# A third weight chunk by seven products, its turns shared with the down-projection, in a float32 decoder layer on one core

## The chip, the cores and the metric

One Trainium2 chip, one of its cores. The metric is the device time of one execution in microseconds (us); lower is better. A core has TensorE (PE, matrix products into PSUM banks), VectorE (DVE), ScalarE (ACT), GpSimd (POOL) and SyncE (SP, which here only starts transfers). They run their own instruction streams, each in its own order, and meet through semaphores.

## The reference

A decoder layer for 256 tokens of width 1024, all in float32:

```python
h = rms_norm(x, norm1_g[l])
proj = h @ w_in[l]                       # attention q, k, v and the convolution's input
...
x = x + jnp.concatenate([attn, conv], axis=-1) @ w_out[l]
h = rms_norm(x, norm2_g[l])
x = x + (jax.nn.silu(h @ w_gate[l]) * (h @ w_up[l])) @ w_down[l]
```

`w_gate` and `w_up` are 1024 x 2816, `w_down` is 2816 x 1024. The change lies in the last line.

## The kernel before

**Products.** Each float32 operand is held as a high part (`h`, the rounded value) and a low part (`l`, the rest). `product` makes three matmuls of 128 x 128 by 128 x 512: high by high, high by low, low by high. Weights come from memory as blocks of 128 x 2048 float32 (`raw`, 1 MB, four buffers) and are split in pieces of 1024 columns: ScalarE writes the high half (`wh`, L256), VectorE the low half (`wl`, L265), into seven pairs of buffers. `feed(at + LEAD)` keeps the split some four pieces ahead of the products. When a block's second piece is split, `load_next` starts the next load on SP's queue.

**Chunks.** The 2816 columns of gate and up are cut in six chunks: five of 512 and chunk 3 of 256. A plain chunk of 512 takes 8 units of 4 products (two token halves, two halves of the contraction, gate and up): 32 products. A unit uses one piece, and all of a chunk's gate or up goes to two banks (`fg`). A *shared* chunk sees tokens by contraction halves (A11 to A22) and weights (b11, b21 of gate, b12, b22 of up) as 2 x 2 matrices and multiplies them with seven block products in place of eight: 7 units of 4 products, into the banks U, V and W. For that, sums of the tokens' blocks (`xs`) are formed once, and sums of weight blocks on the way: VectorE adds b12 and then b22 to b11 (`raw<-raw,raw`, L255, four instructions a chunk), and POOL's queue adds b22 to b12 and b21 to b11 by accumulating transfers (L268). So a shared chunk has 14 pieces. Its b11, b12 and b22 have homes of their own (`big_h`, `big_l`, `side`), b21 a `raw` buffer.

**Order.** `STAGES = ((0,), (1, 2), (3,), (4, 5))`: chunk 0 plain; chunk 1 shared, its units in turns with plain chunk 2; chunk 3; chunk 4 shared, in turns with plain chunk 5. Then come the 22 row tiles of the down-projection, four products a row with one piece, into the four banks pd00 to pd11; the last four rows (`LAST`) are done bank by bank. TensorE's order is that of the code; a task list (`spawn`, `step`, one step each two products) puts the work on finished banks in between: `gate2_task` and `up2_task` for plain chunks (silu on ScalarE, then `ac`, the product with it, on VectorE at L796), and `turned` (four transposes `aT` on TensorE at L787, the high part on ScalarE at L790, the low part `lo` on VectorE at L792).

**Banks.** There are eight: four under `mm`, two under `s`, two under `t`, each dealt out in turn. Before, `fg` and W come from `mm`, U and V from `s`, transposes from `t`; of the pd banks two come from `s` and two from `mm`.

Of the kernel before, what the change touches and what calls it, by code (L numbers as in the profile page):

```python
# [16 lines left out]
P = 128  # L17
# [47 lines left out]
STAGES = ((0,), (1, 2), (3,), (4, 5))  # L65


def _halves(c):

    if c:  # L70
        return [(z, kh, half) for z in range(2) for kh in range(2) for half in range(2)]
    return [(z, kh, half) for kh in range(2) for z in range(2) for half in range(2)]


def _plan():

    base = 14
    block = {}
    for c, width in enumerate(WIDTHS):
        for z in range(2 if width == W else 1):  # L80
            for kh in range(2):
                block[c, z, kh] = base
                base += 1
    loads = [(i, "raw") for i in range(2, 14)]
    plain = lambda i: [(i, a, None, "load") for a in range(2)]
    sources = [p for i in range(14) for p in plain(i)]
    for stage in STAGES:
        second = [(block[stage[-1], z, kh], half) for z, kh, half in _halves(stage[-1])
                  if (stage[-1], z, kh) in block]
        second_pieces = [(i, half, None, "load")  # L90
                         for j, (i, half) in enumerate(second)]
        second_loads = [(i, "raw") for i, half in second if half == 0]
        if len(stage) == 1:
            loads += second_loads
            sources += second_pieces
            continue
        b11, b21, b12, b22 = (block[stage[0], z, kh] for z in range(2) for kh in range(2))
        loads += [(b11, "big_h"), (b12, "big_l"), second_loads[0], second_loads[1], (b22, "side"),
                  (b21, "raw")] + second_loads[2:]
        both = [(0, 1) for _ in range(7)]  # L100
        todo = [(b11, None, None), (b11, b12, (b12, b22)), (b11, b22, (b11, b21)), (b21, None, "load"),
                (b12, None, None), (b22, None, None), (b11, None, None)]
        for j in range(8):
            if j < 7:
                i, add, then = todo[j]
                sources += [(i, a, add, then) for a in range(2)]
            sources.append(second_pieces[j])
    for i in range(base, NB):
        loads.append((i, "raw"))
        sources += plain(i)  # L110
    return loads, sources
# [66 lines left out]
def _build(nc, tc, t, ctx):  # L178
# [18 lines left out]
    def load(pl, name, shape, eng=nc.sync, **kw):  # L197
        tl = pl.tile(shape, F32, name="c_" + name, **kw)
        eng.dma_start(tl, t[name])
        return tl  # L200
# [21 lines left out]
    loads, sources = _plan()  # L222

    def load_next():
        while loads:
            i, home = loads.pop(0)
            if home == "raw":
                r = raw.tile([P, BW], F32, name=f"raw{i}", tag="raw")
            else:
                r = (late_pool[0] if home == "side" else keep).tile([P, BW], F32, name=f"raw{i}", tag=home)  # L230
            nc.sync.dma_start(r, t["w"][i - 2])
            blocks[i] = r
            if home == "raw":
                return
# [14 lines left out]
    def feed(upto):  # L249
# [8 lines left out]
        while waiting and waiting[0][2] <= upto:  # L258
            dst, src, j = waiting.pop(0)
            i, a, add, then = sources[j]  # L260
            if then == "low":
                nc.scalar.activation(dst[1], dst[0].bitcast(F32), AF.Copy, scale=-1.0)
                nc.gpsimd.dma_start(dst[1].bitcast(F32), src, accum_op=ALU.add)
            else:
                nc.vector.tensor_tensor(dst[1], src, dst[0].bitcast(F32), op=ALU.subtract)  # L265
            if type(then) is tuple:
                to, more = then
                nc.gpsimd.dma_start(blocks[to][:, cut(a)], t["w"][more - 2][:, cut(a)], accum_op=ALU.add)  # L268
            if then in ("load", "low") and a:
                load_next()  # L270
# [42 lines left out]
    g1 = load(const, "g1", [P, KT], nc.scalar)  # L313
# [36 lines left out]
    for kt in range(KT):  # L350
# [9 lines left out]
        if kt == 1:  # L360
            load_next()
            rope = load(early, "rope", [P, NT, 2 * HD])
            gqk = load(early, "gqk", [P, 2, 2 * HD])
# [6 lines left out]
    ident = load(const, "ident", [P, P])  # L370
    load_next()
    taps = load(early, "taps", [96, 324], tag="Y", bufs=3)
    dwr = early.tile([96, W], F32, name="dwr", tag="Y", bufs=3)
    nc.sync.dma_start(dwr, t["dw_w"])
    mask = load(early, "mask", [P, 3 * P])
# [18 lines left out]
    def tables_task():  # L394
# [12 lines left out]
        G["glub"] = load(early, "glub", [P, 2, W])  # L407
        G["cols"] = load(const, "cols", [P, 16])
# [307 lines left out]
    def residual_task(i, n):  # L716
        cols = slice(n * W, n * W + W)
        nc.vector.tensor_tensor(x2[:, i, cols], po[i, n], x2[:, i, cols], op=ALU.add)
        sq = ffn["late"].tile([P, W], F32, name=f"sq{i}{n}", tag="sum", bufs=5)
# [50 lines left out]
    acts = late.tile([P, 2, NF, T], F32R, name="act")  # L770

# [32 lines left out]
    def up2_task(c, banks, width):  # L804
        ups = []
        for i in range(NT):
            ups.append(times(c, i, banks[i][:, W - width:] if width < W else banks[i], ffn["s", c][i], width))
            yield 1
        for i in range(NT):
            yield from turned(c, i, ups[i], width // P)  # L810

    def part(name):
        return late.tile([P, W], F32, name=name, tag="sum", bufs=5)

    xs = [acts[:, z, NF - 8:, :].rearrange("p f (b q) -> p (f b) q", b=2).rearrange("p (s k) q -> p s k q", s=4)
          for z in range(2)]

    def xsums_task():
# [3 lines left out]
        for j, (p, q, op) in enumerate(((A21, A22, ALU.subtract), (s[0], A11, ALU.subtract),  # L822
                                        (A11, A21, ALU.subtract), (A12, s[1], ALU.add))):
            nc.vector.tensor_tensor(s[j], p, q, op=op)
        yield 1
        for j in range(4):
            nc.scalar.activation(xs[0][:, j], s[j], AF.Copy)
        yield 2
        for j in range(4):
            nc.vector.tensor_tensor(xs[1][:, j], s[j], xs[0][:, j].bitcast(F32), op=ALU.subtract)  # L830
# [36 lines left out]
    xsum = lambda j: [[z[:, j, k, :] for z in xs] for k in range(4)]  # L867

    def plain_units(c):

        banks = {}

        def unit(z, kh, half):
            if kh == half == 0:
                banks[z] = [mm_bank(f"fg{c}{z}{i}") for i in range(NT)]
            for k in (2 * half, 2 * half + 1):
                if k % 2 == 0:
                    feed(at[0] + LEAD)
                for i in range(NT):
                    product(banks[z][i], [a[:, 4 * kh + k, tok(i)] for a in g], wpart(at[0], k % 2),  # L880
                            kh == k == 0, kh == 1 and k == 3)
            at[0] += 1
            if kh == half == 1:
                spawn((gate2_task, up2_task)[z](c, banks[z], W), EVICT)

        return [lambda z=z, kh=kh, half=half: unit(z, kh, half) for z, kh, half in _halves(c)]

    def shared_units(c):

        U, V = (t_bank(f"{n}{c}", "s") for n in "UV")  # L890
        banks = {"U": U, "V": V}

        def unit(lhs, name, start, stop, after):
            if name == "W":
                banks["W"] = mm_bank(f"W{c}")
            for k in range(4):
                if k % 2 == 0:
                    feed(at[0] + LEAD)
                product(banks[name], lhs[k], wpart(at[0], k % 2), start and k == 0, stop and k == 3, not start)
                at[0] += k % 2  # L900
            if after:
                spawn(after(), EVICT)

        todo = ((block(0, 0), "U", True, True, lambda: copied("s1", U)),
                (xsum(0), "V", True, True, lambda: copied("s5", V)),
                (xsum(1), "U", False, True, lambda: copied("s2", U)),
                (block(1, 0), "W", True, True, lambda: gate_first(c, banks["W"])),
                (xsum(2), "U", False, True, lambda: up_second(c, U)),
                (xsum(3), "V", False, True, lambda: up_first(c, V)),
                (block(1, 1), "U", False, True, lambda: gate_second(c, U)))  # L910
        return [lambda u=u: unit(*u) for u in todo]
# [3 lines left out]
    at = [at]  # L915
    for stage in STAGES:
        if len(stage) == 2:
            first, second = shared_units(stage[0]), plain_units(stage[1])
            for j in range(8):
                if j < 7:  # L920
                    first[j]()
                second[j]()
        elif WIDTHS[stage[0]] == W:
            for u in plain_units(stage[0]):
                u()
        else:
            c = stage[0]
            banks = [mm_bank(f"fg{c}{i}") for i in range(NT)]
            for k in range(KT):
                if k % 2 == 0:  # L930
                    feed(at[0] + k // 2 + LEAD)
                for i in range(NT):
                    product(banks[i], [a[:, k, tok(i)] for a in g], wpart(at[0] + k // 2, k % 2), k == 0, k == KT - 1)
# [75 lines left out]
```

## Time and profile before

| | |
|---|---|
| median of 3 runs | 294.79 us (294.23 to 295.06) |
| profiled execution | 294.38 us, span 292.4 us |
| TensorE | 285.6 us busy, 1333 matmuls |
| VectorE | 213.1 us busy, 326 instructions |
| ScalarE | 174.1 us busy, 262 instructions |
| transfers | 60.73 MB, 208 GB/s over the span |

Times in the profile are us from the span's start. A duration of a matmul contains part of its neighbour's, since TensorE overlaps them; the chain of waits lists each stretch of work on the path to the end once, with its time. `aT<-c_ident,ac` reads: written `aT`, from `c_ident` and `ac`. `[0.87 <-DVE ac L796]` is idle time of the engine just before, and what ended it.

### The profile page before, as it was taken

What the parts mean: (1) busy time and instruction counts of PE and PEld (TensorE: products, weight loads), DVE (VectorE), ACT (ScalarE), POOL (GpSimd) and SP (SyncE); (2) the same over time, 40 slices, a digit from 0 to 9 for tenths busy, and PEclk for the clock granted to TensorE, in tenths of its full rate; (3) what the DMA queues carried; (4) which work ended last, traced back from release to release, by engine and by line L of the source; (5) the groups of instructions that cost most, each with busy time, mean ns of one, the idle gap of its engine ahead of it and who ended that gap; (6) DMA issues with size and microseconds to landing.
All of it is one profiled execution on the core that took longest, in us unless ns stands there. A gap on an engine that the chain in (4) does not pass through costs nothing.

```text
span 292.4 us, 3667 instructions
## 1 busy us (share of the span) xinstructions
PE 285.6 (98%) x1333; PEld 231.6 (79%) x1333; DVE 213.1 (73%) x326; ACT 174.1 (60%) x262; POOL 21.4 (7%) x42
## 2 busy tenths in 40 slices
PE   8999999999999999997999999999999999999994
PEld 6888877778688888885888888888888888888883
DVE  3899995999972957999987758997787574544111
ACT  5776768989825778655967454597856263343000
POOL 0005372000000000021100001120000000000000
PEclk9999999999999999999999999999999999999999
DMA  7999868533703439299961993899335368400012
GB/s 250 416 411 364 337 250 308 210 143 146 288 0 143 146 108 429 84 388 240 213 266 45 427 422 119 143 244 320 132 133 189 133 226 323 164 2 0 0 48 96
DMA packets 11475, 60.73 MB, mean 208 GB/s; under 512 B 1537, under 2 KB 2145, under 8 KB 5698
## 3 DMA queue, kind: packets, MB, share of 16 engines
q1 hardware_dynamic: 9874, 54.86, 49.1%
q0 software_dynamic: 1440, 5.64, 9.5%
q8 instruction: 10, 0.16, 0.2%
q14 instruction: 7, 0.06, 0.1%
q10 hardware_dynamic: 144, 0.00, 0.0%
HBM read 59.46 MB, written 1.05 MB: 207 GB/s over the span
## 4 chain that ended last, share of the span: by engine, by line
PE 84%; DVE 10%; ACT 2%; issue 2%; DVEq 0%; ACTq 0%
PE pd L708 21%; PE p L669 18%; PE fg L708 18%; PE po L708 7%; PE U L708 7%; PE V L708 3%; DVE wl L265 3%; PE W L708 2%; DVE raw L255 2%; PE aT L787 2%; PE warm L326 1%; PE S L512 1%; PE pT L542 1%; ACT wh L256 1%; DVE g L735 1%
## 5 line engine op out<-in xcount | busy, mean ns | idle before, releaser
L265 DVE TENSOR_TENSOR wl<-raw,wh 128x1024 fp32r<-128x1024 f32 x102 | 122.7, 1221 | 24.4 <-ACT wh L256 24.0
L256 ACT ACTIVATE wh<-raw 128x1024 fp32r<-128x1024 f32 x102 | 105.9, 1056 | 46.3 <-PE pd L708 19.9
L708 PE MATMUL fg<-wh,g 128*128 128x512 f32 x224 | 72.8, 392 | 0.0
L708 PE MATMUL pd<-wh,act 128*128 128x512 f32 x176 | 55.2, 391 | 0.0
L708 PEld LDWEIGHTS fg<-wh,g 128*128 128x128 f32 x224 | 42.0, 188 | 8.6
L708 PE MATMUL fg<-wl,g 128*128 128x512 f32 x112 | 43.6, 389 | 0.0
L708 PEld LDWEIGHTS pd<-wh,act 128*128 128x128 f32 x176 | 33.0, 188 | 6.9
L708 PE MATMUL pd<-wl,act 128*128 128x512 f32 x88 | 34.2, 389 | 0.0
L669 PE MATMUL p<-wh,xh 128*128 128x512 f32 x80 | 32.9, 412 | 0.0
L669 PE MATMUL p<-wh,xl 128*128 128x512 f32 x80 | 31.3, 392 | 0.0
L669 PE MATMUL p<-wl,xh 128*128 128x512 f32 x80 | 26.5, 392 | 0.0
L708 PEld LDWEIGHTS fg<-wl,g 128*128 128x128 f32 x112 | 21.1, 188 | 4.2
L708 PEld LDWEIGHTS pd<-wl,act 128*128 128x128 f32 x88 | 16.5, 188 | 3.3
L669 PEld LDWEIGHTS p<-wh,xh 128*128 128x128 f32 x80 | 15.1, 189 | 3.7 <-issue 0.7
L669 PEld LDWEIGHTS p<-wl,xh 128*128 128x128 f32 x80 | 15.1, 189 | 3.1 <-DVE wl L265 0.2
L669 PEld LDWEIGHTS p<-wh,xl 128*128 128x128 f32 x80 | 15.1, 188 | 3.1
L790 ACT ACTIVATE act<-aT 128x512 fp32r<-128x512 f32 (+1 forms) x12 | 6.7, 561 | 17.9 <-PE aT L787 17.9
L268 POOL DMA_DIRECT2D raw<-w x8 | 7.0, 879 | 141.4 <-DVE raw L255 86.4
L792 DVE TENSOR_TENSOR act<-aT,act 128x512 fp32r<-128x512 f32 (+1 forms) x12 | 7.7, 644 | 11.4 <-ACT act L790 11.4
L948 DVE TENSOR_TENSOR o<-pd,x 128x512 f32<-128x512 f32 x4 | 2.8, 692 | 14.6 <-PE pd L708 14.6
L708 PE MATMUL po<-wh,mixh 128*128 128x512 f32 x32 | 12.6, 395 | 0.0
L708 PE MATMUL po<-wh,mixl 128*128 128x512 f32 x32 | 12.5, 390 | 0.0
(169 smaller groups left out, 374.8 us busy)
## 6 DMA issues: line engine op xcount, KB each, us to landing
raw<-w SPq DMA_DIRECT2D x45, 1024.0 KB, 5.2
raw<-w POOLq DMA_DIRECT2D x8, 512.0 KB, 7.0
first<-first SPq DMA_DIRECT2D x8, 384.0 KB, 6.1
xtok<-xtok SPq DMA_DIRECT2D x2, 512.0 KB, 9.0
x<-xtok SPq DMA_DIRECT2D x2, 512.0 KB, 6.2
out<-o SPq DMA_DIRECT2D x4, 256.0 KB, 2.0
inv<-inv POOLq DMA_DIRECT2D x1, 768.0 KB, 7.0
fwd<-fwd POOLq DMA_DIRECT2D x1, 648.0 KB, 4.2
```

What stands on the lines that cost most here:

```text
L255: nc.vector.tensor_tensor(src, src, blocks[add][:, cut(a)], op=ALU.add)
L256: nc.scalar.activation(dst[0], src, AF.Copy)
L265: nc.vector.tensor_tensor(dst[1], src, dst[0].bitcast(F32), op=ALU.subtract)
L268: nc.gpsimd.dma_start(blocks[to][:, cut(a)], t["w"][more - 2][:, cut(a)], accum_op=ALU.add)
L326: nc.tensor.matmul(warm[:, 0:T], zeros[:, 0:P], zeros, start=True, stop=True)
L512: nc.tensor.matmul(banks[a][:, out], G["qT"][rows, j, q], G["kT"][rows, j, k], start=True, stop=True)
L542: nc.tensor.transpose(b[:, a * P:(a + 1) * P], p[:, a * P:(a + 1) * P], ident)
L669: nc.tensor.matmul(banks[i], (xh, xh, xl)[a][:, kt, sls[i]], w[a % 2], start=kt == 0 and a == 0, stop=kt == KT - 1 and a == 2 - (order[-1] ...
L708: nc.tensor.matmul(bank, l, r, start=start and a == 0, stop=stop and a == 2, skip_group_check=on)
L787: nc.tensor.transpose(b[:, a, :], u[:, a * P:(a + 1) * P], ident)
L790: nc.scalar.activation(hi, b[:, 0:nf, :], AF.Copy)
L792: nc.vector.tensor_tensor(lo, b[:, 0:nf, :], hi.bitcast(F32), op=ALU.subtract)
```

## The change

1. Chunk 5 becomes shared as well (`SHARED = (1, 4, 5)`): 7 units in place of 8, 14 pieces in place of 8, with its own additions and accumulating transfers.
2. A single list, `_order()`, sets the sequence: chunk 0; chunk 1 in turns with plain chunk 2; chunk 3; stage 4, that is chunk 4 in turns with rows 0 to 7 of the down-projection; stage 5, chunk 5 in turns with rows 8 to 15; rows 16 to 21.
3. The pd banks are therefore taken when row 0 starts, all four from `mm`; W moves from `mm` to `t`.
4. The homes go round (`HOMES`): as a home's last piece is split, the block of the next shared chunk that takes it is loaded, by a call at that place and no longer from the common list.
5. Of the tokens' sums half lie in a tile of their own (`xs`, named `more` in the code); the rows of `act` that held them are used earlier now. `sum` has four buffers in place of five.
6. `FIRST_TURN = 3`: chunk 0's transposes come three steps (six products) later.

```diff
-STAGES = ((0,), (1, 2), (3,), (4, 5))
+SHARED = (1, 4, 5)
+HOMES = ("big_h", "big_l", "side")
+FIRST_TURN = 3
...
+def _order():
+    chunk = lambda c: [("g", c, z, kh, a) for z in range(2) for kh in range(2) for a in range(2)]
+    rows = lambda a, b: [("f", f) for f in range(a, b)]
+    order = [("g", 0, z, kh, a) for kh in range(2) for z in range(2) for a in range(2)]
+    def stage(c, others):
+        for j in range(8):
+            if j < 7:
+                order.append(("s", c, j))
+            order.append(others[j])
+    stage(1, chunk(2))
+    order.extend(("h", 3, 0, kh, a) for kh in range(2) for a in range(2))
+    stage(4, rows(0, 8))
+    stage(5, rows(8, 16))
+    return order + rows(16, NF)
...
+        after = (None,) * 4 if n + 1 == len(SHARED) else quarters[n + 1]
+        i, add, more, then = ((b11, None, None, None), (b11, b12, (b12, b22), None), (b11, b22, (b11, b21), None),
+                              (b21, None, None, "load"), (b12, None, None, after[0]), (b22, None, None, after[2]),
+                              (b11, None, None, after[3]))[j]
...
     acts = late.tile([P, 2, NF, T], F32R, name="act")
+    load(first_shared[0])
+    load(first_shared[2])
...
             ups.append(times(c, i, banks[i][:, W - width:] if width < W else banks[i], ffn["s", c][i], width))
             yield 1
+        yield 0 if c else FIRST_TURN
         for i in range(NT):
             yield from turned(c, i, ups[i], width // P)
...
-            if name == "W":
-                banks["W"] = mm_bank(f"W{c}")
+        if j == 3:
+            Wb[c] = t_bank(f"W{c}")
...
-    pd = {(i, n): t_bank(f"pd{i}{n}", "s") if i == 0 else mm_bank(f"pd{i}{n}") for i in range(NT) for n in range(2)}
+    def row(f, i, n, w):
+        if f == 0:
+            pd[i, n] = mm_bank(f"pd{i}{n}")
+        product(pd[i, n], [acts[:, z, f, tok(i)] for z in range(2)], w, f == 0, f == NF - 1)
```

How the instructions move is shown at three places. In the rows, `aT01` is the transpose bank of chunk 0, token half 1; `wh39` and `wl39` are the two halves of piece 39; `g2` are the tokens. First TensorE in the stage of chunks 1 and 2, at chunk 0's transposes, before:

```order
L708 MATMUL fg201_1417<-wh38_1330,g2_1081 128x512
L787 MATMUL aT00_1438<-c_ident_168,ac00_1414 128x128 x4
L708 MATMUL V1_1389<-wh39_1348,act_1186 128x512
L708 MATMUL V1_1389<-wl39_1349,act_1186 128x512
L708 MATMUL V1_1389<-wh39_1348,act_1186 128x512 x2
L708 MATMUL V1_1389<-wl39_1349,act_1186 128x512
L708 MATMUL V1_1389<-wh39_1348,act_1186 128x512
L787 MATMUL aT01_1458<-c_ident_168,ac01_1430 128x128 x4
L708 MATMUL V1_1389<-wh40_1370,act_1186 128x512
```

And the transposes' place now:

```order
L723 MATMUL fg201_1424<-wh41_1389,g2_1081 128x512
L804 MATMUL aT00_1472<-c_ident_168,ac00_1415 128x128 x4
L723 MATMUL fg200_1423<-wh41_1389,g2_1081 128x512
L723 MATMUL fg200_1423<-wl41_1390,g2_1081 128x512
L723 MATMUL fg200_1423<-wh41_1389,g2_1081 128x512
L723 MATMUL fg201_1424<-wh41_1389,g2_1081 128x512
L723 MATMUL fg201_1424<-wl41_1390,g2_1081 128x512
L723 MATMUL fg201_1424<-wh41_1389,g2_1081 128x512
L804 MATMUL aT01_1485<-c_ident_168,ac01_1431 128x128 x4
L723 MATMUL U1_1394<-wh42_1402,act_1182 128x512
```

The transposes moved from ahead of V's unit (pieces 39 and 40) to the middle of the plain unit behind it (piece 41): 18 matmuls further on.

Second TensorE one unit into the stage of chunk 4, with the semaphores that an instruction waits for, before (`fg500` and `fg501` are chunk 5's gate banks):

```order
L708 MATMUL fg500_1861<-wh64_1764,g2_1081 128x512 [waits Activation_49]
L708 MATMUL fg500_1861<-wl64_1765,g2_1081 128x512 [waits DVE_49]
L708 MATMUL fg500_1861<-wh64_1764,g2_1081 128x512
L708 MATMUL fg501_1862<-wh64_1764,g2_1081 128x512
L708 MATMUL fg501_1862<-wl64_1765,g2_1081 128x512
```

And now:

```order
L723 MATMUL pd00_1868<-wh64_1765,act_1182 128x512 [waits Activation_49]
L723 MATMUL pd00_1868<-wl64_1766,act_1182 128x512 [waits DVE_49]
L723 MATMUL pd00_1868<-wh64_1765,act_1182 128x512
L723 MATMUL pd01_1872<-wh64_1765,act_1182 128x512
L723 MATMUL pd01_1872<-wl64_1766,act_1182 128x512
L723 MATMUL pd01_1872<-wh64_1765,act_1182 128x512
L723 MATMUL pd10_1878<-wh64_1765,act_1182 128x512 [waits DVE_49,PE_49]
L723 MATMUL pd10_1878<-wl64_1766,act_1182 128x512
L723 MATMUL pd10_1878<-wh64_1765,act_1182 128x512
L723 MATMUL pd11_1882<-wh64_1765,act_1182 128x512 [waits DVE_49]
```

Row 0 of the down-projection stands where chunk 5's first plain unit stood; the first matmuls into pd10 and pd11 wait for VectorE, beside the waits for piece 64 that were there before.

Third VectorE at the end of chunk 4, from its last but one bank on, before (`ac40` and `ac41` are chunk 4's two products with silu, `aT40` and `aT41` their transposes, `ac50` chunk 5's):

```order
L796 SCALAR_TENSOR_TENSOR ac40_2105<-c124_2103,rstd2_1265,sg04_2027 128x512
L265 TENSOR_TENSOR wl84_2086<-raw36_1940,wh84_2085 128x1024
L265 TENSOR_TENSOR wl85_2108<-raw36_1940,wh85_2107 128x1024
L265 TENSOR_TENSOR wl86_2118<-raw37_1952,wh86_2117 128x1024
L792 TENSOR_TENSOR act_1186<-aT40_2129,act_1186 128x4x128
L265 TENSOR_TENSOR wl87_2136<-raw37_1952,wh87_2135 128x1024
L796 SCALAR_TENSOR_TENSOR ac41_2166<-c224_2063,rstd2_1265,sg14_2152 128x512
L265 TENSOR_TENSOR wl88_2155<-raw38_2033,wh88_2154 128x1024
L792 TENSOR_TENSOR act_1186<-aT41_2188,act_1186 128x4x128
L796 SCALAR_TENSOR_TENSOR ac50_2201<-fg510_2045,rstd2_1265,sf50_2041 128x512
```

And now:

```order
L277 TENSOR_TENSOR wl85_2111<-raw32_1985,wh85_2110 128x1024
L271 TENSOR_TENSOR raw32_1985<-raw32_1985,raw34_2026 128x1024
L277 TENSOR_TENSOR wl86_2121<-raw40_1943,wh86_2120 128x1024
L809 TENSOR_TENSOR act_1182<-aT40_2130,act_1182 128x4x128
L271 TENSOR_TENSOR raw32_1985<-raw32_1985,raw34_2026 128x1024
L277 TENSOR_TENSOR wl87_2137<-raw32_1985,wh87_2136 128x1024
L813 SCALAR_TENSOR_TENSOR ac41_2168<-c224_2064,rstd2_1264,sg14_2154 128x512
L277 TENSOR_TENSOR wl88_2157<-raw32_1985,wh88_2156 128x1024
L271 TENSOR_TENSOR raw32_1985<-raw32_1985,raw35_2070 128x1024
L277 TENSOR_TENSOR wl89_2177<-raw40_1943,wh89_2176 128x1024
L809 TENSOR_TENSOR act_1182<-aT41_2189,act_1182 128x4x128
L271 TENSOR_TENSOR raw32_1985<-raw32_1985,raw35_2070 128x1024
```

The four additions of chunk 5's blocks (`raw32<-raw32,...`) now stand between the low halves and chunk 4's last work on banks; pieces 84 to 88 are chunk 5's and one row's, where all were rows of the down-projection.

More of the change, by code (lines that the diff above doesn't have):

```diff
@@ L83, in _plan @@
                 base += 1
[L84 to L95, printed above, removed]
-            continue
[L97 to L111, printed above, removed]
+    loads, sources, homes = list(range(2, 14)), [], {}
+    for i in range(14):
+        sources += [(i, 0, None, ()), (i, 1, None, (("load",),))]
+    quarters = [[block[c, z, kh] for z in range(2) for kh in range(2)] for c in SHARED]
+    for n, (b11, b21, b12, b22) in enumerate(quarters):
+        for j, b in enumerate((b11, b12, b22)):
+            homes[b] = HOMES[(n + j) % 3]
@@ L114, in _round12 @@
+    return loads, sources, homes, quarters[0]
 def _round12(a):
@@ L221, in _build, with load @@
     blocks, pieces = {}, []
-    loads, sources = _plan()
-    def load_next():
[L225 to L234, printed above, removed]
+    loads, sources, homes, first_shared = _plan()
+    def load(i):
+        if i in homes:
+            pl = late_pool[0] if homes[i] == "side" else keep
+            r = pl.tile([P, BW], F32, name=f"raw{i}", tag=homes[i])
+        else:
+            r = raw.tile([P, BW], F32, name=f"raw{i}", tag="raw")
+        nc.sync.dma_start(r, t["w"][i - 2])
+        blocks[i] = r
+    def load_next():
+        if loads:
+            load(loads.pop(0))
     def split(dst, src, eng):
@@ L260, in feed @@
             i, a, add, then = sources[j]
[L261 to L270, printed above, removed]
+            nc.vector.tensor_tensor(dst[1], src, dst[0].bitcast(F32), op=ALU.subtract)
+            for what, *args in then:
+                if what == "load":
+                    load_next()
+                elif what == "home":
+                    load(args[0])
+                else:
+                    to, more = args
+                    nc.gpsimd.dma_start(blocks[to][:, cut(a)], t["w"][more - 2][:, cut(a)], accum_op=ALU.add)
     def wpart(j, a):
@@ L866, in _build @@
     block = lambda kh, i: [[z[:, 4 * kh + k, tok(i)] for z in g] for k in range(4)]
[L867 to L883, printed above, removed]
-                spawn((gate2_task, up2_task)[z](c, banks[z], W), EVICT)
-        return [lambda z=z, kh=kh, half=half: unit(z, kh, half) for z, kh, half in _halves(c)]
@@ L888, in shared_units @@
[L888 to L893, printed above, removed]
-            if name == "W":
-                banks["W"] = mm_bank(f"W{c}")
[L896 to L911, printed above, removed]
+    xsum = lambda j: [[z[j][:, k, :] for z in xs] for k in range(4)]
@@ new lines, in _build, with plain_unit @@
+    U, V, Wb, banks = {}, {}, {}, {}
+    def plain_unit(c, z, kh, half):
+        if kh == half == 0:
+            banks[z] = [mm_bank(f"fg{c}{z}{i}") for i in range(NT)]
+        for k in (2 * half, 2 * half + 1):
+            for i in range(NT):
+                product(banks[z][i], [a[:, 4 * kh + k, tok(i)] for a in g], wpart(at, k % 2),
+                        kh == k == 0, kh == 1 and k == 3)
+        if kh == half == 1:
+            if WIDTHS[c] == W:
+                spawn((gate2_task, up2_task)[z](c, banks[z], W), EVICT)
+            else:
+                spawn(gate2_task(c, banks[0], T), EVICT)
+                spawn(up2_task(c, banks[0], T), EVICT + 1)
@@ L913, in _build @@
+    pd = {}
+    def row(f, i, n, w):
+        if f == 0:
+            pd[i, n] = mm_bank(f"pd{i}{n}")
+        product(pd[i, n], [acts[:, z, f, tok(i)] for z in range(2)], w, f == 0, f == NF - 1)
     spawn(norm2_task(), SS_WAIT)
     spawn(xsums_task(), SUMS_WAIT)
[L915 to L925, printed above, removed]
-        else:
[L927 to L933, printed above, removed]
-            at[0] += 4
-            spawn(gate2_task(c, banks, T), EVICT)
-            spawn(up2_task(c, banks, T), EVICT + 1)
@@ L938, in _build @@
[L938 to L947 removed]
+    last = {}
@@ new lines, in _build @@
+    for kind, *unit in _order():
+        feed(at + LEAD)
+        if kind in "gh":
+            plain_unit(*unit)
+        elif kind == "s":
+            shared_unit(*unit)
+            at += 1
+        elif unit[0] < NF - LAST:
+            for i in range(NT):
+                for n in range(2):
+                    row(unit[0], i, n, wpart(at, n))
+        else:
+            last[unit[0]] = at
+        at += 1
+    for i in range(NT):
+        for n in range(2):
+            for f in range(NF - LAST, NF):
+                row(f, i, n, wpart(last[f], n))
+            o = late.tile([P, W], F32, name=f"o{i}{n}", tag="sum", bufs=4)
```

76 lines of the change are left out of this document (48 added, 28 removed).

## The prediction

> **What bounds the kernel now.** I read the page's busy shares first, then the chain of waits, then busy time by stretch.
>
> ```profile
> span 292.4 us, 3667 instructions
> ...
> PE 285.6 (98%) x1333; PEld 231.6 (79%) x1333; DVE 213.1 (73%) x326; ACT 174.1 (60%) x262; POOL 21.4 (7%) x42
> ...
> PE 84%; DVE 10%; ACT 2%; issue 2%; DVEq 0%; ACTq 0%
> ```
>
> TensorE is busy nearly always and carries 84% of the chain. The page's 0.39 us for one matmul is no price, since neighbours overlap. The price is in the chain:
>
> ```profile
> 137.47 0.67 DVE ac L796
> 138.15 0.04 issue
> 138.19 0.66 PE aT L787 x4
> ...
> 185.67 2.72 PE U L708 x12
> 188.39 2.72 PE fg L708 x12
> ...
> 228.82 0.44 PE aT L787 x4
> ...
> 235.65 53.09 PE pd L708 x234
> ```
>
> 53.09 / 234 = 0.227 us a matmul, so a product costs 0.68 us, a unit of four products 2.72, and four transposes 0.44 where nobody waits. From 138.19 to the last matmul the chain is TensorE alone; ahead of that the first chunk's transposes hang on VectorE. By stretch, in the columns stretch, length, then busy time (and instructions) of PE, PEld, DVE, ACT, POOL, clock, DMA share and GB/s:
>
> ```profile
> 128.80:138.20 9.40, 7.66 (x36) 5.76 (x34) 9.35 (x10) 5.61 (x8) 1.32 (x2) 1.00 1.04 253
> ...
> 185.67:227.46 41.79, 41.79 (x189) 34.52 (x189) 34.38 (x35) 28.69 (x35) 1.74 (x2) 1.00 0.65 199
> 227.46:289.00 61.54, 61.27 (x277) 50.37 (x275) 26.08 (x26) 18.32 (x19) 0.00 (x0) 1.00 0.29 109
> ```
>
> The first stretch has VectorE full and TensorE with holes. The second is the stage that holds chunk 4 by seven products: VectorE at 34.4 of 41.8 us, TensorE without a hole. The third is the down-projection, where VectorE has 35 us to spare. So a matmul removed after 138 us is worth its 0.227 us, unless something else then makes TensorE wait.
>
> **The change, part by part.**
>
> *Fewer products.* Chunk 5 goes from 8 units to 7: 12 matmuls at 0.227 us are **−2.72 us**. All else on TensorE keeps its count.
>
> *The first chunk's transposes.* These rows are TensorE's, in the columns start, duration, instruction and the idle time ahead:
>
> ```profile
> 134.00 0.39 PE L708 MATMUL fg<-wh,g 128*128 128x512 f32 x1
> 135.26 0.66 PE L787 MATMUL aT<-c_ident,ac 128*128 128x128 f32 x4 [0.87 <-DVE ac L796]
> 135.67 0.49 PE L708 MATMUL V<-wh,act 128*128 128x512 f32 x1
> 136.00 0.40 PE L708 MATMUL V<-wl,act 128*128 128x512 f32 x1
> ...
> 138.19 0.66 PE L787 MATMUL aT<-c_ident,ac 128*128 128x128 f32 x4 [0.87 <-DVE ac L796]
> ```
>
> From the matmul at 134.00 to the one at 136.00 go 2.00 us; unhindered it would be two pitches and the transposes, 0.23 + 0.44 + 0.23 = 0.90. So a wait costs 1.1 us and the two of them 2.2. Moved behind 18 matmuls (4.08 us), the first pair's four transposes come at about 134.23 + 4.08 = 138.3 and the second four, six matmuls and four transposes on, at 140.1. What they need:
>
> ```profile
> 134.46 0.74 DVE L796 SCALAR_TENSOR_TENSOR ac<-fg,rstd,sf 128x512 f32<-128x512 f32 x1
> ...
> 137.39 0.74 DVE L796 SCALAR_TENSOR_TENSOR ac<-fg,rstd,sf 128x512 f32<-128x512 f32 x1
> 138.05 1.22 DVE L265 TENSOR_TENSOR wl<-raw,wh 128x1024 fp32r<-128x1024 f32 x1
> ```
>
> Both `ac` are there by 138.13, ahead of 138.3 and 140.1: no wait, **−2.2 us**. What is late next? VectorE is full until past 142, and TensorE now wants its weights up to 2.2 us sooner. The low half that the next U unit needs (one piece ahead of the `wl` at 138.05) is done by 137.4, and U starts at 140.6; the one at 138.05 is done at 139.2 and wanted at 141.9. Some 2.7 us are left. The bank of W, now shared with the transposes, waits for `lo` of the first row: three `wl` behind 138.05, about 142, against W's start at 146.0. Bounds: 0 (all of it paid elsewhere) to −2.2; I take −2.2, because each date above has room.
>
> *The down-projection's banks.* This is the new wait. The four pd banks are taken from the four `mm` buffers when row 0 starts, one unit into stage 4. The first two were chunk 2's up banks, read by 179. The other two, pd10 and pd11, were chunk 3's and are free only when VectorE has done `ac30` and `ac31`. The order has a wait for VectorE at both, and none at this place before. VectorE's rows ahead of them, TensorE's first matmul of the unit that stands there now, and the two `ac` by form:
>
> ```profile
> 182.21 0.69 DVE L792 TENSOR_TENSOR act<-aT,act 128x512 fp32r<-128x512 f32 x1 [0.39 <-ACT act L790]
> 182.82 1.22 DVE L255 TENSOR_TENSOR raw<-raw,raw 128x1024 f32<-128x1024 f32 x1
> ...
> 189.77 1.22 DVE L265 TENSOR_TENSOR wl<-raw,wh 128x1024 fp32r<-128x1024 f32 x1
> 190.91 0.87 DVE L796 SCALAR_TENSOR_TENSOR ac<-fg,rstd,sf 128x256 f32<-128x256 f32 x2
> ...
> 188.23 0.39 PE L708 MATMUL fg<-wh,g 128*128 128x512 f32 x1
> ...
> L796 DVE SCALAR_TENSOR_TENSOR ac<-fg,rstd,sf 128x256 f32<-128x256 f32 x2 | 0.9, 476 | 0.0
> ```
>
> VectorE runs without a gap from 182.21 to 190.91, released by transposes that TensorE did just before, and its order there is unchanged; so it moves along with TensorE and stays as late as it is. pd10 is wanted 6 matmuls after 188.23, at 189.59. `ac30` ends at 190.91 + 0.48 = 191.39; the handover at 135.26 came 0.06 after its `ac` ended (134.46 + 0.74). So pd10 starts at 191.45: **+1.86 us**, and everything behind it on TensorE's queue waits along, U, V and the later rows. pd11 comes 0.68 later, when `ac31` (191.78) is done. Bounds: 0, if the banks fall otherwise, to 2.5, if `ac31` decides pd10 too and the handover takes its share.
>
> The Trainium skill ("TensorE: Matmul & The Clock Gate", "The HAM clock gate") says that the clock halves only after an idle window of about 3.4 us; 1.86 would not reach that, and the sum stays. Its section "A second HAM failure mode: psum-queue depth-cycling" has short idles between bank groups dropping the clock all the same. The trace leans to the first: two holes of 0.87 us within 3 us, and the stretch 128.80:138.20 has clock 1.00.
>
> *More work for VectorE and ScalarE.* VectorE gets 13 instructions: 6 low halves, 4 additions of blocks, 3 on banks. ScalarE gets 9: 6 high halves and 3 copies. At VectorE's pitch of 1.14 (189.77 to 190.91) and at most 0.69 for a bank operation that is 10 × 1.14 + 3 × 0.69 = 13.5 us. Stage 5 then has what stage 4 had, 34.4 us in 41.8, and the whole tail 26.1 + 13.5 = 39.6 in about 58. Cost 0, hidden by TensorE, as stage 4 in the second stretch shows it. If the cover went, it would be at the start of stage 5, where four additions stand between low halves. The same place without the additions:
>
> ```profile
> 217.52 3.65 DVE L265 TENSOR_TENSOR wl<-raw,wh 128x1024 fp32r<-128x1024 f32 x3
> 222.64 0.69 DVE L792 TENSOR_TENSOR act<-aT,act 128x512 fp32r<-128x512 f32 x1 [1.47 <-ACT act L790]
> ...
> 224.73 0.75 DVE L796 SCALAR_TENSOR_TENSOR ac<-c,rstd,sg 128x512 f32<-128x512 f32 x1
> ...
> 229.93 0.69 DVE L792 TENSOR_TENSOR act<-aT,act 128x512 fp32r<-128x512 f32 x1 [3.32 <-ACT act L790]
> ```
>
> In these times stage 5 starts at 227.46. Adding the new rows in order: `ac41` ends at about 226.2 (its transposes come at 228.8), the second `lo` stays at 229.9, the fourth addition ends at 231.7, the low half behind it at 232.8; its matmuls come four units and 0.44 after 227.46, at 238.8. 6 us of room.
>
> *Transfers.* Three blocks of chunk 5 are loaded as homes come free in stage 4, and POOL gets 4 more accumulating transfers.
>
> ```profile
> raw<-w SPq DMA_DIRECT2D x45, 1024.0 KB, 5.2
> raw<-w POOLq DMA_DIRECT2D x8, 512.0 KB, 7.0
> ...
> DMA to landing us min/median/max: 4.7/5.2/11.7
> ```
>
> The tightest is the second home, free at about 207.0 in the times above and wanted by the first addition at 219.8: 12.8 us against a longest of 11.7. The third has 212.5 to 226.2. The accumulated blocks are wanted 8 units after the stage starts, 21.8 us, against 7.0 and a start ahead of it. Cost 0. On SP's queue the first home's load still stands until the output projection is done, but the two raw loads that stood behind it now go ahead of it and come earlier; nobody waits for that. Four `sum` buffers in place of five cost 0, since each is read a unit or more before it comes round again.
>
> *The tail.* Between chunk 5's last unit and its use there were 42 us, now there are four rows. Its second transposes come 0.44 + 2.72 + 2.72 + 1.36 = 7.2 us after that unit; their `lo` ends 2.0 later (in the rows above 229.93 + 0.69, for transposes at 228.66), and one more low half, that of the last row, ends at 10.4. It is wanted after transposes, four rows and three products, 0.44 + 10.88 + 2.04 = 13.4. Cost 0, with 3 us of room.
>
> Sum: −2.72 − 2.2 + 1.86 = **−3.06 us**. The profiled execution took 294.38 us (its span 292.4 and 2 us around it), 0.41 below the median of 294.79. So 291.3 against its own time, and **291.7** as a median.
>
> **The rivals.**
>
> 1. *No wait at pd10.* For it: the ring of banks could be dealt out otherwise. Against: the order's waits. 291.7 − 1.9 = 289.9.
> 2. *Stage 5 late by VectorE or a home.* For it: 12.8 against 11.7 us above. Against: 6 us between an addition and its matmuls, and stage 4 without a hole. A loss of one addition's pitch or two, 1 to 2 us: 293.
> 3. *The transposes' gain is paid elsewhere,* since VectorE is full until 142. Half of it left: 292.8; none: 293.9.
> 4. *Slower: chunk 5's third home.* Its addition stands ahead of every later low half on VectorE. It may start 5.2 us (two additions, two low halves, one `lo`) before its matmuls at 238.8, at 233.6; with 212.5 that allows a landing of 21 us. Each us beyond costs one, and from 24 us on the change is slower: 26 us would give 291.7 + 5 = 296.7. Against: the longest of 45 loads is 11.7.
> 5. *The clock drops at the hole.* The start-up row below has the array slow: 18 matmuls of 256 columns in 4.02 us, 223 ns each, where 512 take 227 later. A stretch as long at half rate loses 2 us: 293.7. This is the Trainium skill's second section above at work; no hole in this trace shows it.
>
> ```profile
> 1.04 4.02 PE L326 MATMUL warm<-zeros 128*128 128x256 bf16 x18 [1.04 <-DVE one L309]
> ```
>
> **How the numbers follow.** Forecast 0.62, rival 1 0.12, rival 2 0.11, rival 3 0.08, rival 4 0.04, rival 5 0.03. The range goes from rival 1 to past rival 2 and half of rival 3: 289.7 to 293.3, leaving out rival 4, 5 and the worse ends of 2 and 3. Within 0.3% means 293.9 to 295.7. Faster: 0.62 + 0.12 + 0.10 + 0.05 + 0.01 = 0.90; same 0.06; slower 0.04.
>
> **What would show it.** 1321 matmuls. No idle before `aT` at 135 to 141. One hole on TensorE of 1.7 to 2 us before pd in row 0, released by VectorE's `ac` of 256 columns, and none in stage 5. Clock 1.00 through it. It would be wrong with a hole in stage 5, an addition waiting for a transfer, or low halves late at 140 to 146.

## The result, and the profile after

The changed kernel takes **292.1 us** (291.87 to 292.33 in 4 runs), beside 294.51 (294.21 to 295.06 in 4 runs) for the kernel before in the same series: a ratio of 0.9916 [0.9897, 0.9936], 2.4 us. The forecast was 291.7, its range 289.7 to 293.3. Of the experiments' runs, one of the 12 of experiment 1 took 733.23 us; the ratio there leaves it out. The profiled execution after took 291.87 us, its span 290.1. From the page of after, the span, the busy times and the shares of the chain:

```profile
span 290.1 us, 3686 instructions
...
PE 282.8 (97%) x1321; PEld 229.8 (79%) x1321; DVE 226.3 (78%) x339; ACT 181.8 (63%) x271; POOL 24.9 (9%) x46
...
PE 92%; DVE 3%; DMA 1%; issue 1%; ACT 1%; SPq 0%; ACTq 0%
```

There are 12 matmuls fewer, and TensorE's share of the chain rises from 84% to 92%: the start of chunk 1's stage hangs on VectorE no longer. TensorE's waits after, in the columns engine, line waited for, then us in total, times, longest:

```profile
PE pd L723 <- DVE ac L813: 1.8, 1, 1.8
PE warm L341 <- DVE one L324: 1.0, 1, 1.0
PE cv L296 <- DVE yl L254: 0.2, 1, 0.2
```

The other two belong to work ahead of the change and stand in the kernel before too. The two waits of `aT` for `ac` are gone, and one wait has come. TensorE's rows after, at chunk 0's transposes and at pd10 (start, duration, instruction, idle time ahead):

```profile
138.13 0.39 PE L723 MATMUL fg<-wh,g 128*128 128x512 f32 x1
138.36 0.60 PE L804 MATMUL aT<-c_ident,ac 128*128 128x128 f32 x4
138.71 0.48 PE L723 MATMUL fg<-wh,g 128*128 128x512 f32 x1
...
140.19 0.60 PE L804 MATMUL aT<-c_ident,ac 128*128 128x128 f32 x4
...
187.25 0.39 PE L723 MATMUL pd<-wh,act 128*128 128x512 f32 x1
189.42 0.47 PE L723 MATMUL pd<-wh,act 128*128 128x512 f32 x1 [1.78 <-DVE ac L813]
```

The transposes start at 138.36 and 140.19 (forecast: 138.3 and 140.1), a pitch behind the matmul ahead of them. pd10 starts 2.17 us after the matmul ahead of it where a pitch is 0.227, hence 1.94 late. VectorE's rows after, for the same two places and for the start of stage 5:

```profile
137.44 0.74 DVE L813 SCALAR_TENSOR_TENSOR ac<-fg,rstd,sf 128x512 f32<-128x512 f32 x1
138.10 3.49 DVE L277 TENSOR_TENSOR wl<-raw,wh 128x1024 fp32r<-128x1024 f32 x3
141.50 0.68 DVE L809 TENSOR_TENSOR act<-aT,act 128x512 fp32r<-128x512 f32 x1
...
187.66 1.22 DVE L277 TENSOR_TENSOR wl<-raw,wh 128x1024 fp32r<-128x1024 f32 x1
188.79 0.87 DVE L813 SCALAR_TENSOR_TENSOR ac<-fg,rstd,sf 128x256 f32<-128x256 f32 x2
...
219.71 1.22 DVE L271 TENSOR_TENSOR raw<-raw,raw 128x1024 f32<-128x1024 f32 x1
...
225.43 0.74 DVE L813 SCALAR_TENSOR_TENSOR ac<-c,rstd,sg 128x512 f32<-128x512 f32 x1
...
230.45 1.22 DVE L271 TENSOR_TENSOR raw<-raw,raw 128x1024 f32<-128x1024 f32 x1
231.59 1.22 DVE L277 TENSOR_TENSOR wl<-raw,wh 128x1024 fp32r<-128x1024 f32 x1
```

`ac30` is the first half of the pair at 188.79; with the 0.48 us of one it ends at 189.27, and pd10 starts 0.15 later. By stretch (stretch, length, busy time and instructions of PE, PEld, DVE, ACT, POOL, clock, DMA share, GB/s), the start of chunk 1's stage, stage 4, and all behind it up to the last `o`:

```profile
128.80:138.20 9.40, 9.40 (x43) 7.77 (x43) 9.35 (x10) 5.62 (x8) 1.27 (x2) 1.00 0.92 203
183.40:227.38 43.98, 42.20 (x190) 34.63 (x189) 36.97 (x38) 28.06 (x33) 3.49 (x4) 1.00 0.82 241
227.38:286.20 58.82, 58.58 (x264) 48.16 (x263) 37.05 (x37) 26.88 (x30) 1.75 (x2) 1.00 0.36 110
```

TensorE does 43 matmuls and transposes in the 9.40 us where it did 36; stage 4 has one hole of 1.78 (43.98 - 42.20); stage 5 and the rows behind it have none while TensorE works. The clock is 1.00 in all three.

### The profile page after: what moved, and what is told of

Its sections match the earlier page's. It is cut to its first block, busy times and chain, and to the rows that moved or that the text cites. A ratio compares the mean times of both kernels' runs of the same rounds, so it can differ in the third digit from the quotient of the medians.

```text
span 290.1 us, 3686 instructions
## 1 busy us (share of the span) xinstructions
PE 282.8 (97%) x1321; PEld 229.8 (79%) x1321; DVE 226.3 (78%) x339; ACT 181.8 (63%) x271; POOL 24.9 (9%) x46
## 4 chain that ended last, share of the span: by engine, by line
PE 92%; DVE 3%; DMA 1%; issue 1%; ACT 1%; SPq 0%; ACTq 0%
PE pd L723 20%; PE p L684 18%; PE fg L723 17%; PE U L723 10%; PE po L723 8%; PE V L723 6%; PE W L723 3%; PE aT L804 2%; DMA Y<-dw_b 1%; PE warm L341 1%; PE S L527 1%; DVE wl L277 1%; PE pT L557 1%; DVE raw L271 1%; PE x2T L746 1%
## 5 line engine op out<-in xcount | busy, mean ns | idle before, releaser
L277 DVE TENSOR_TENSOR wl<-raw,wh 128x1024 fp32r<-128x1024 f32 x108 | 129.5, 1221 | 11.4 <-ACT wh L272 10.9
L272 ACT ACTIVATE wh<-raw 128x1024 fp32r<-128x1024 f32 x108 | 111.8, 1057 | 35.6 <-DVE raw L271 12.5
L723 PE MATMUL pd<-wh,act 128*128 128x512 f32 x176 | 57.4, 393 | 1.8 <-DVE ac L813 1.8
L723 PE MATMUL fg<-wh,g 128*128 128x512 f32 x160 | 52.1, 394 | 0.0
L723 PEld LDWEIGHTS fg<-wh,g 128*128 128x128 f32 x160 | 30.1, 188 | 6.1
L723 PE MATMUL fg<-wl,g 128*128 128x512 f32 x80 | 31.2, 390 | 0.0
L285 POOL DMA_DIRECT2D raw<-w x12 | 10.5, 876 | 179.5 <-DVE raw L271 118.4
L723 PEld LDWEIGHTS fg<-wl,g 128*128 128x128 f32 x80 | 15.1, 188 | 2.9
L723 PE MATMUL U<-wh,g 128*128 128x512 f32 x48 | 16.1, 392 | 0.0
L271 DVE TENSOR_TENSOR raw<-raw,raw 128x1024 f32<-128x1024 f32 x12 | 14.6, 1218 | 0.0
```

Of the source, the lines that this page charges most:

```text
L271: nc.vector.tensor_tensor(src, src, blocks[add][:, cut(a)], op=ALU.add)
L272: nc.scalar.activation(dst[0], src, AF.Copy)
L723: nc.tensor.matmul(bank, l, r, start=start and a == 0, stop=stop and a == 2, skip_group_check=on)
```

## The experiments

In each diff `-` is the kernel named and `+` the experiment. Times are medians. Runs of the kernel before that stood beside them had medians of 294.75 in the first series (the first four experiments), 294.57 in the second, 294.65 in the third (the last four). The changed kernel was not run again beside them, so a difference to it is taken between two gains, each over the kernel before in its own series; the changed kernel's is 2.4 us. "The end" is the time from the start of the last `o` on VectorE to the end of the span.

**1. The transposes at their old place.** The changed kernel with:

```diff
-FIRST_TURN = 3
+FIRST_TURN = 0
```

> The changed kernel with FIRST_TURN = 0: chunk 0's transposes back ahead of V's unit, all else as changed. Theory (two waits of 1.1 us at the transposes were removed by the later place and nothing was paid for it): TensorE idles twice for about 0.87 us before aT at 134 to 139, the wait at pd10 stays at 1.8, and the time is 2.0 to 2.2 us above the changed kernel's 292.1, about 294.2. Rival (VectorE was full there, so the gain was mostly paid elsewhere): at most 1 us above, 292.1 to 293.1.

Measured: 294.43 us, ratio to before 0.9983 [0.9975, 0.9992]. TensorE's waits:

```profile
PE pd L723 <- DVE ac L813: 1.8, 1, 1.8
PE aT L804 <- DVE ac L813: 1.8, 2, 0.9
```

Both waits are back, and 2.1 us with them: without `FIRST_TURN` the change as a whole wins 0.3 us in place of 2.4.

**2. Only the later transposes.** The kernel before with:

```diff
             yield 1
+        yield 0 if c else 3
         for i in range(NT):
             yield from turned(c, i, ups[i], width // P)
```

> The kernel before with the later transposes alone (three steps for chunk 0). Theory: the parts add up, so this alone gives 2.0 to 2.2 us: 292.3 to 292.5, with no wait of TensorE left between 104 us and the end. Rival (the whole change's net gain of 2.4 us comes from the products removed, and the transposes matter little): 293.5 to 294.5.

Measured: 292.7 us, ratio 0.9926 [0.9911, 0.994], -2.05 us. TensorE's waits:

```profile
PE warm L326 <- DVE one L309: 1.0, 1, 1.0
PE cv L281 <- DVE yl L238: 0.2, 1, 0.2
```

So most of the result is this one line. The third shared chunk, which is nearly all of the diff, adds 0.4 us to it (2.4 - 2.05; the two medians alone differ by 0.6).

**3. The wait at pd10, by an earlier `ac30`.** The changed kernel with chunk 3's work on its banks a step or two sooner:

```diff
-            yield 1
-        yield 0 if c else FIRST_TURN
+            yield 0 if c == 3 else 1
+        yield (FIRST_TURN, 0, 0, 3, 0, 0)[c]
...
-                spawn(up2_task(c, banks[0], T), EVICT + 1)
+                spawn(up2_task(c, banks[0], T), EVICT)
```

> The changed kernel, with both of VectorE's ac of chunk 3 put one addition and one low half earlier in its order (its transposes stay where they are). Theory (pd10's bank is chunk 3's and the hole is VectorE's lateness with ac30): ac ends at about 187.6 and 188.0 in place of 189.3 and 189.7, the hole of 1.78 us before pd shrinks to about 0.1 to 0.2, and the time is 1.7 to 1.9 us below the changed kernel: 290.2 to 290.4. Rival (the hole is only where a lateness of the stage shows, so it comes up again in the additions or low halves behind it): 291.5 to 292.1, with a new hole in stage 4.

Measured: 290.3 us, ratio 0.9852 [0.9835, 0.9868]. The chain of waits (start, duration) at row 0, and VectorE's row:

```profile
183.37 2.72 PE U L723 x12
186.09 2.96 PE pd L723 x12
189.05 1.38 PE V L723 x6
...
186.85 0.88 DVE L813 SCALAR_TENSOR_TENSOR ac<-fg,rstd,sf 128x256 f32<-128x256 f32 x2 [0.43 <-ACT sf L798]
```

The pair of `ac` starts 1.94 us sooner than after (186.85 against 188.79), and row 0 takes 2.96 us, 0.24 above a row's 2.72. The gain is 4.45 us, 2.0 more than the changed kernel's. So the wait was VectorE's lateness with `ac30`, and no new one came in stage 4.

**4. The wait at pd10, by later rows.** The changed kernel with two units ahead of row 0 in stage 4, and the last two rows of the stage at its end:

```diff
+        if c == 4:
+            order.extend([("s", c, 0), ("s", c, 1), others[0]])
+            for j in range(2, 7):
+                order.extend([("s", c, j), others[j - 1]])
+            order.extend(others[6:])
+            return
```

> The changed kernel, with stage 4's rows of the down-projection one shared unit later (two shared units ahead of row 0, rows 6 and 7 together at the end). Theory: row 0 wants its banks 2.72 us later while chunk 3's banks come free at about the same time, so no hole before pd: 290.1 to 290.4. Rival (two shared units in a row ask VectorE for the additions sooner and the hole moves to V or U): 291 to 292.5.

Measured: 289.9 us (289.62 to 290.18), ratio 0.983 [0.9815, 0.9845]. The chain at row 0:

```profile
183.59 2.72 PE U L729 x12
186.31 2.72 PE V L729 x12
189.03 1.36 PE pd L729 x6
190.39 0.22 PE aT L810 x2
```

No wait is left at row 0. The gain is 4.85 us, 2.4 more than the changed kernel's.

**5. Stage 5's units back to back.** The changed kernel with:

```diff
-    stage(5, rows(8, 16))
-    return order + rows(16, NF)
+    order.extend(("s", 5, j) for j in range(7))
+    return order + rows(8, NF)
```

> The changed kernel, but stage 5's seven shared units stand back to back and rows 8 to 21 behind them: in these units no row of the down-projection stands between two units as cover for VectorE. Theory (stage 5 has room: VectorE's 14 low halves at 1.14, four additions at 1.22 and some banks' operations, about 22.5 us from 217.4, still end ahead of each unit): 291.8 to 292.4 us, no hole over 0.5 us in stage 5. Rival (the turns with the rows are what pays for VectorE's additional work; without them 22.5 us of VectorE stand against 19 us of TensorE): holes of 1 to 3 us in U, V or W, 293 to 295.

Measured: 292.13 us, ratio 0.9916 [0.9902, 0.993]. The chain at two of the units, and the stretch of the seven units:

```profile
230.70 2.74 PE V L723 x12
233.44 2.92 PE U L723 x12
...
244.52 2.82 PE U L723 x12
...
227.50:246.50 19.00, 19.00 (x87) 15.29 (x86) 18.57 (x19) 16.86 (x20) 1.75 (x2) 1.00 0.57 144
```

The theory held. But VectorE is busy 18.57 of 19.00 us here, and two units take 0.20 and 0.10 us more than 2.72: stage 5 can do without the turns with the rows, but only just.

**6 and 7. How much room stage 5 has.** The changed kernel with some low halves written twice, the same values; the limit is 86 in the first and 88 in the second:

```diff
-            nc.vector.tensor_tensor(dst[1], src, dst[0].bitcast(F32), op=ALU.subtract)
+            for _ in range(2 if 84 <= j < 86 else 1):
+                nc.vector.tensor_tensor(dst[1], src, dst[0].bitcast(F32), op=ALU.subtract)
```

> The changed kernel with the low halves of two pieces at the start of stage 5 (84 and 85) written twice, the same values: 2 x 1.14 = 2.28 us more on VectorE there. Theory: the prediction's room of 6 us for low halves is not the tight place; chunk 4's last ac ends at 226.17 and its transposes start at 228.74, so 2.3 us later it is still ahead of them: 292.1 us, at most +0.2. Rival (no room at all, each us of VectorE there costs one): 294.4.

> As the one with two low halves written twice, but four (pieces 84 to 87): 4 x 1.14 = 4.56 us more on VectorE at the start of stage 5. Theory: the room there is that of chunk 4's last transposes, 228.74 - 226.17 = 2.6 us, so they wait 2.0 us for VectorE's ac and the time is 294.1. Rival (the room is the 6 us that the prediction gave for the low half behind the fourth addition): 292.1, no wait.

Measured: 291.94 us with two (0.9907 [0.9893, 0.992]). With four the median is 295.73, of two sorts: 293.99 to 294.36 in four runs at a mean clock of 0.997 to 0.999, and 295.5 to 296.8 in seven at 0.992 or 0.993. With four, in an execution of the first sort, TensorE's rows and VectorE's at chunk 4's last transposes:

```profile
228.64 0.39 PE L724 MATMUL U<-wh,g 128*128 128x512 f32 x1
230.98 0.66 PE L805 MATMUL aT<-c_ident,ac 128*128 128x128 f32 x4 [1.95 <-DVE ac L814]
...
230.18 0.74 DVE L814 SCALAR_TENSOR_TENSOR ac<-c,rstd,sg 128x512 f32<-128x512 f32 x1
```

The theory held for that sort: the tight place of stage 5 is not the low half with its 6 us but `ac41`, 2.6 us ahead of its transposes. The second sort neither theory had.

**8 and 9. The end of the span.** The end takes 4.10 us after and 3.68 before (the spans, 290.10 and 292.44, less the start of the last `o`; the rows stand below, with the sum). From the first to the second of GpSimd's closing semaphore instructions it is 430 ns after and 78 before. First the kernel before with four small loads (8 KB each) on GpSimd's queue, then with eight small instructions on GpSimd:

```diff
+    extra = late.tile([P, 4, 16], F32, name="extra")
+    for j in range(4):
+        nc.gpsimd.dma_start(extra[:, j], t["cols"])
```

```diff
+    extra = late.tile([P, 8], F32, name="extra")
+    nc.gpsimd.memset(extra, 0.0)
+    for j in range(7):
+        nc.gpsimd.tensor_scalar(extra, extra, 1.0, 1.0, op0=ALU.mult, op1=ALU.add)
```

> The kernel before with four more small loads on GpSimd's queue (4 KB each or so, of columns that nobody reads), hence 14 transfers on that queue's software path as in the changed kernel, in place of 10. It asks why the span ends 4.06 to 4.11 us after the last addition o starts in the changed kernel and 3.68 in the one before. Theory (the closing of GpSimd's stream grows with its transfers): 4.1 us, +0.4 in all. Rival (it hangs on something else in the change): 3.7, no change.

> The kernel before with eight small instructions on GpSimd (a memset and seven tensor_scalar of 8 columns, on a tile nobody reads) and no transfer more. Again the end of the span: 0.35 us of pause stands between two of GpSimd's closing semaphore instructions in the changed kernel and not in the one before, and four more transfers did not bring it. Theory (it hangs on how many instructions GpSimd's stream holds, so on where the closing ones stand in it): the end comes 4.1 us after the last o starts. Rival (the number has no part in it): 3.7.

Measured: 294.51 us (0.9998 [0.9989, 1.0007]) and 294.44 in one run; the end 3.7 us in both. So the number of transfers is not the cause, and eight instructions more did not bring the pause either: neither theory held.

**10. The same eight instructions in the changed kernel.**

```diff
+    extra = late.tile([P, 8], F32, name="extra")
+    nc.gpsimd.memset(extra, 0.0)
+    for j in range(7):
+        nc.gpsimd.tensor_scalar(extra, extra, 1.0, 1.0, op0=ALU.mult, op1=ALU.add)
```

> The changed kernel with eight small instructions on GpSimd (a memset and seven tensor_scalar), no transfer more. Theory (the pause of 0.35 us before the end hangs on where GpSimd's closing instructions stand in its stream, so it can move away as well as come): the end comes 3.7 us after the last o starts. Rival (it belongs to the changed kernel whatever GpSimd's stream holds): 4.1.

Measured: 291.88 us in one run. GpSimd's closing semaphore instructions, first after and then here (line, engine's queue, operation, count: shortest/median/longest ns, first and last start):

```profile
L1008 POOLq EVENT_SEMAPHORE  x4: 17/17/17, 289.0 to 290.0; - x4
```

```profile
L1012 POOLq EVENT_SEMAPHORE  x4: 17/17/17, 289.4 to 290.0; - x4
```

From the first to the last of the four it is 1.0 us after and 0.6 here, and the end is 290.1 - 286.42 = 3.7 us. The theory held as far as one execution shows it: the pause went when GpSimd's stream was changed. One thing more goes with it: in each of the nine traces with the pause a transfer of 8 KB starts on the instruction queue q14 within 0.05 us of the span's end, and in none of the five without it. It starts some 0.7 us behind the pause, so it is a sign of where the closing stands in the program as that is loaded, and not shown to be the cause. The time did not fall, though, for the last `o` starts 0.42 us later. Part of that shows in the chain, where four units take 2.79 us instead of 2.72, among them these two:

```profile
207.97 2.79 PE U L723 x12
...
213.50 2.79 PE V L723 x12
```

Why they do, no run here tells.

**11 and 12. The clock.** Experiment 3 with the low halves of pieces 84 to 87 written twice, then of 84 to 88: one hole in place of the two of experiment 7.

```diff
-            nc.vector.tensor_tensor(dst[1], src, dst[0].bitcast(F32), op=ALU.subtract)
+            for _ in range(2 if 84 <= j < 88 else 1):
+                nc.vector.tensor_tensor(dst[1], src, dst[0].bitcast(F32), op=ALU.subtract)
```

> The version with chunk 3's work earlier (no wait at pd10), and in it the low halves of pieces 84 to 87 written twice. With the changed kernel as the base this gave two sorts of runs: 294.0 to 294.4 us, and 295.5 to 296.8 at a mean clock of 0.992. Here the wait of 1.8 us at pd10 is gone and only the one of 1.9 us at chunk 4's last transposes is left. Theory (the clock drops after that one hole by itself, in some executions): runs near 290.3 + 2.0 = 292.3, and others near 294.2 at a mean clock of 0.992. Rival (it takes both holes): all near 292.3, clock 0.997 or above.

> As the version with chunk 3's work earlier and four low halves written twice, but five (pieces 84 to 88): 1.14 us more, so the one hole at chunk 4's last transposes is some 3.0 us long. Theory (the clock drops after a hole of this length, the oftener the longer it is): 293.4 us in runs at full clock, 295.3 or more with the clock lost, and the second sort more frequent than with four. Rival (the clock does not hang on the hole's length): 293.4 in all or in the same share of the runs.

Measured: 292.58 us with four (292.30 to 292.69 in 4 runs, clock 0.997 to 0.999). With five 292.79: seven runs at 292.09 to 293.06 with clock 0.997 to 0.999, three at 294.04 to 295.10 with 0.991 to 0.994. The hole is the same in both, against the expectation; first with four, then with five:

```profile
229.28 0.66 PE L805 MATMUL aT<-c_ident,ac 128*128 128x128 f32 x4 [1.95 <-DVE ac L814]
```

```profile
229.03 0.66 PE L805 MATMUL aT<-c_ident,ac 128*128 128x128 f32 x4 [1.95 <-DVE ac L814]
```

The fifth low half stands behind `ac41` on VectorE, so it could not lengthen the hole, and the expectation of 3.0 us was wrong. What the pair does show: the loss of clock needs no wait at pd10, since three of ten runs of the last kernel have it, and its profiled execution has no such wait. Whether it comes oftener after longer holes was not tested, nor was VectorE's additional work without a hole.

## Why the prediction was right, point by point

The forecast was -3.06 us for one execution; the spans differ by 292.44 - 290.10 = 2.34. Four rows of each timeline cut the span in pieces: the first matmul of chunk 1's stage, of stage 4 and of the stage behind it, and the last `o`. Before:

```profile
128.79 0.39 PE L708 MATMUL U<-wh,g 128*128 128x512 f32 x1
...
185.51 0.39 PE L708 MATMUL U<-wh,g 128*128 128x512 f32 x1
...
227.30 0.39 PE L708 MATMUL pd<-wh,act 128*128 128x512 f32 x1
...
288.76 0.69 DVE L948 TENSOR_TENSOR o<-pd,x 128x512 f32<-128x512 f32 x1 [2.03 <-PE pd L708]
```

And after:

```profile
128.84 0.39 PE L723 MATMUL U<-wh,g 128*128 128x512 f32 x1
...
183.40 0.39 PE L723 MATMUL U<-wh,g 128*128 128x512 f32 x1
...
227.22 0.39 PE L723 MATMUL U<-wh,g 128*128 128x512 f32 x1
...
286.00 0.69 DVE L952 TENSOR_TENSOR o<-pd,x 128x512 f32<-128x512 f32 x1 [2.03 <-PE pd L723]
```

| piece | step | before | after | measured | forecast |
|---|---|---|---|---|---|
| ahead of chunk 1 | none | 128.79 | 128.84 | +0.05 | 0 |
| chunk 1 to stage 4 | chunk 0's transposes | 56.72 | 54.56 | -2.16 | -2.2 |
| stage 4 | the wait at pd10 | 41.79 | 43.82 | +2.03 | +1.86 |
| to the last `o` | chunk 5's 12 matmuls | 61.46 | 58.78 | -2.68 | -2.72 |
| the end | none | 3.68 | 4.10 | +0.42 | 0 |
| sum | | 292.44 | 290.10 | -2.34 | -3.06 |

- *Fewer products.* Right, without a hole from stage 5 on. VectorE's 13 and ScalarE's 9 instructions more cost nothing, as said.
- *The transposes.* Right in size and in both dates. Experiments 1 and 2 give it from two sides, 2.1 and 2.05. What was feared to be late next was not: of the three `wl` from 138.10 on the first ends at 139.3, and U wanted it at 141.9.
- *The wait at pd10.* Right in place, in releaser and nearly in size. The term was 0.17 us too small; 0.09 of that is the handover after `ac30`, taken as 0.06 us from `aT`, where it took 0.15; the other 0.08 was not traced. Rival 1 (no wait) is refuted; experiments 3 and 4 remove the wait and win 2.0 and 2.4 us.
- *Stage 5.* The fourth addition ends at 231.67 and the low half behind it at 232.81, as worked out (231.7, 232.8). The first addition started at 219.71, the date on which the second home was wanted, with no idle time ahead of it. But the room named, 6 us, was that of the wrong wait: `ac41`, whose two dates the prediction had (226.2 and 228.8), has 2.6, and experiments 6 and 7 find the edge between 2.3 and 4.6 us of added work. That the cost came out as 0 was luck in so far as the place that decides was not the one that had been worked out. Rivals 2, 3 and 4 did not happen; the longest landing of a raw block after was 10.9 us.
- *The step that failed:* the sum has no term for the end of the span, which grew by 0.42 us. Experiment 8 rules out the number of GpSimd's transfers, experiment 9 the eight instructions by themselves; experiment 10 points to where GpSimd's closing stands in its stream, and the cause stays open.
- *The clock (rival 5).* It stayed at 1.00 after the hole of 1.78 us, as forecast. The profile's rows give 1.00 for the start-up stretch too, so the half rate that the rival takes from it rests on durations alone. Yet the rival is not without substance: in experiments 7, 11 and 12, with a hole of 1.95 us in the profiled executions, 10 of 25 runs took 1.3 to 2.6 us more at a lower mean clock, and 0.006 of 294 us (0.998 to 0.992) is 1.8 us. The Trainium skill ("TensorE: Matmul & The Clock Gate", "The HAM clock gate") asks for an idle window of about 3.4 us. The traces here show less: in experiment 7's the clock is 1.00 at 290.6 us and 0.50 from 290.7 on, and the last matmul ended at 288.43, only 2.2 us before. The Trainium skill's section "A second HAM failure mode: psum-queue depth-cycling" speaks of frequent short idles; experiment 12's profiled execution has one hole.
- *What the traces show of the clock beyond that.* In all fourteen the record of the clock stands at 1.00 for 283.31 or 286.72 us, which is 83 or 84 times 3.413, and at 0.50 from there on, always behind the last matmul. Cut the time into stretches of 3.413 us, counted back from that change. In the last stretch ahead of it TensorE was idle for 2.20 us or more; in no stretch before that for more than 1.79, and none of those was followed by half clock. If an edge between these two is the rule, a hole of 1.78 us does nothing, and one of 1.95 us may count where it falls whole into one stretch. That would be 1.46 of 3.41 us, 43% of the time, and half clock for one stretch would cost 1.7 us; 10 of 25 runs were slower, by 1.3 to 2.6. This is an estimate from the ends of the traces. No run that lost clock on the way was profiled, so where the clock fell in it, and that the hole made it fall, is not shown.

The profiled execution took 291.87 us where 291.3 was worked out: 0.72 more of span, less 0.17 of time around the span (1.77 against 1.94). The median is 0.4 above its forecast, but the gain is 0.65 short of it (2.41 against 3.06): the kernel before took 294.51 in this series, and 294.79 in the one that the forecast started from. So 0.28 us of the forecast's nearness is luck.

## What to carry to other kernels

Where banks change hands, date the last reader of the old use as closely as the first writer of the new one: here 2.0 us of a gain of 2.7 went to a wait for one small `ac`, and putting one unit of other work in between (experiment 4) brought it back. Room for added work on an engine is the smallest room of all the dates behind it on that engine's queue, not that of the step in question. A large change is best split at once: one line of this one was worth 2.05 us, and the rest 0.3 to 0.6. And a small difference is best taken against a kernel that ran in the same series: the kernel before moved by 0.3 us between two of them.

## What the runs showed of the hardware

- The end of the span is not a constant: 3.7 us in five kernels here and 4.1 in nine, by a pause of some 0.35 us between the first two of GpSimd's closing semaphore instructions. Eight instructions more on GpSimd took it away in the changed kernel, and a block of 8 KB on the instruction queue at the end of the span goes with it; the cause is open.
- TensorE can lose clock, about 1.8 us of time, in some executions of kernels whose profiled execution has a single hole of 1.95 us (3 of 10 runs of one, none of 4 of another); with 1.78 us no run of the changed kernel and its near variants (24 runs) went below a mean clock of 0.997.
- At the end of the traces the clock goes to half 2.2 to 5.0 us after the last matmul, a whole number of stretches of 3.413 us after it became full. That fits a count of idle time in such stretches, with an edge between 1.79 and 2.20 us; ahead of the last matmul no trace here shows it.
